# Sums of weight blocks by copies and adding transfers of the DMA, and one pair of modulation vectors summed on VectorE

## The chip, the core and the metric

The kernel runs on one core of a Trainium2 chip. The metric is the device time of one execution in microseconds (us), lower is better. A core has five engines with a queue each, which run in order: TensorE (PE, matrix products into PSUM), VectorE (DVE), ScalarE (ACT), GpSimd (POOL) and SyncE (SP, which here issues transfers). Sixteen DMA engines carry the transfers that SyncE and GpSimd issue.

## What is computed

One inference step of a small two-layer transformer (depth 2, width 1024) over 512 latent tokens and 128 prompt tokens. Each layer has a mixer and a feed-forward part, and both are modulated: six vectors per layer, of which the first two (shift and scale ahead of the mixer) matter here.

```python
def modulation(cond, w_mod, b_mod):
    m = jax.nn.silu(cond) @ w_mod + b_mod              # (1024,) @ (1024, 6 * 1024)
    return m.reshape(cond.shape[:-1] + (N_MOD, D_MODEL))

def trunk_layer(x, mod, p, lam_init, ctx):
    shift1, scale1, gate1, shift2, scale2, gate2 = [mod[:, i][:, None] for i in range(N_MOD)]
    h = rms_norm(x, p["g_pre_mix"]) * (1.0 + scale1) + shift1
    m, own = mixer_block(h, p, lam_init, ctx)
    x = x + gate1 * rms_norm(m, p["g_post_mix"])
    h = rms_norm(x, p["g_pre_ffn"]) * (1.0 + scale2) + shift2
    f = (jax.nn.silu(h @ p["w_gate"]) * (h @ p["w_up"])) @ p["w_down"]   # width 2816
    x = x + gate2 * rms_norm(f, p["g_post_ffn"])
```

All arrays are fp32. There are two conditions, one for the latent tokens and one for the prompt.

## The kernel before

Tokens stand in five tiles of 128 (640 columns, halves of 320). Most products are made of three matmuls on operands split into a high and a low part (`mm3`, `product`): a block of weights is loaded to `raw` (three buffers), ScalarE writes the high half `wh` (L125) and VectorE the low half `wl` (L121), four buffers each (`piece`, L981 to L987). SyncE issues every transfer, in one queue.

The feed-forward part (`ffn`) runs over 22 blocks of the hidden width, taken in pairs, in four groups (`GROUPS`): pairs 0 and 1, then three groups of three. Group 0 is computed plainly. For groups 1 to 3 the gate and up products of a pair use a scheme of seven products instead of eight (`product` with n = 1 to 7, L1046 to L1048), on four weight blocks and on four sums of them; with b11, b12, b21, b22 the blocks of `w_gu`, the sums are b11+b12, b12+b22, b11+b12+b22 and b11+b12+b21+b22, kept in the DRAM tensor `wsum` (quarters 0, 3, 1, 2). Each group ends with its down projection: for two halves of the output and five token tiles, 12 (group 0) or 18 matmuls of 512 columns (L190 to L192) into one of two PSUM banks in turn, evicted by ScalarE in group 0 and added by VectorE (L1200) in the others.

`sums` (L989) is a generator that makes `wsum` for the next group while the current one runs: for each pair and each half of the columns, four loads of 128x512 to `s` buffers (eight of these exist), four adds on VectorE (L1001), four stores (L1002). `step` advances it by one at chosen places: behind three of the plain products, behind a pair, and behind every tile of the down projection. `step(pre, 1, mark)` also says behind which instruction of an engine the new ones are queued: the last one traced so far on the engines named in `mark`, here VectorE.

The modulation vectors are matrix products with two columns (`c2`, the two conditions, padded to 32). Vectors 0 and 1 of layer 1 are made in the feed-forward part of layer 0, in group 1, by `mod_s` (L335): for eight k and four column blocks a load of 128x512 and one plain fp32 matmul (L342) into 32 of the 128 partitions of one bank, 32 in all; `mod_finish` copies the bank out (L258), transposes it in four pieces (L261) and writes the columns `mc` (L268, L270). `middle` advances it at three places within a pair. The order of instructions on each engine is worked out ahead of time by the compiler's scheduler, within the orders that the program asks for.

Of the kernel before, what the change touches and what calls it, by code (L numbers as in the profile page):

```python
# [10 lines left out]
AF = mybir.ActivationFunctionType  # L11
ALU = mybir.AluOpType
# [3 lines left out]
D = 1024  # L16
NT = 5
TOK = NT * 128
KT = D // 128
# [43 lines left out]
class Kernel:  # L63
# [142 lines left out]
    def consts(self):  # L206
        nc, cp, V, G, SY, a = self.nc, self.cp, self.V, self.G, self.SY, self.a
        t = lambda shape, tag, dt=F32: self.tl(cp, shape, tag, 1, dt)

        self.c2 = t([128, 2 * KT + 30], "c2")  # L210
        V.memset(self.c2, 0.0)
        cc = self.c2[:, 0:2 * KT]
        SY.dma_start(cc, a["c2"])
        th = self.tl(self.wp, [128, 2 * KT], "raw", 3)
        self.S.activation(th, cc, AF.Tanh, scale=0.5)
        V.scalar_tensor_tensor(cc, th, 1.0, cc, op0=ALU.add, op1=ALU.mult)
        V.tensor_scalar(cc, cc, 0.5, None, op0=ALU.mult)
# [12 lines left out]
        self.invcnt = t([128, NT, 4], "invcnt")  # L230
        self.gA = t([128, 4, NT, 64], "gA")
        self.mc = t([128, DEPTH, 4, KT, 2], "mc")
        bg = self.tl(self.wp, [128, 1024], "raw", 3)[:, 0:128]
        SY.dma_start(bg, a["mod_bg"])
        p = self.p("pt")[:, 0:128]
        self.T.transpose(p, bg, self.ident)
        self.bgc = t([128, 128], "bgc")
        self.S.activation(self.bgc, p, AF.Copy)

        V.tensor_scalar(self.bgc[:, 96:128], self.bgc[:, 96:128], math.sqrt(D), None, op0=ALU.mult)  # L240
# [91 lines left out]
            return next(raw) if what == "raw" else self.tl(self.pa, [128, 512], "s", NS, dt)  # L332
        return al

    def mod_s(self, l, pair, p, bank):  # L335

        src = self.a["w_mod"][l].rearrange("(k p) (i n) -> p k i n", p=128, n=D)
        for k in range(KT):
            for j in range(4):
                raw = self.s()  # L340
                self.SY.dma_start(raw, src[:, k, pair[j // 2], j % 2 * 512:(j % 2 + 1) * 512])
                self.T.matmul(p[32 * j:32 * j + 32], self.c2[:, 2 * k:2 * k + 32], raw, start=k == 0, stop=k == KT - 1)  # L342
            yield
        self.mod_finish(l, pair, 512, 0, p, lambda what: self.s(), bank)
        yield

    def row(self, l, i, c, tile_):
# [460 lines left out]
    def mixer_e(self, l, first):  # L808
# [7 lines left out]
        pt = lambda dt=F32: self.tl(pa, [128, NT, 256], "PT", 4, dt)  # L816

        def bg():
            if True:
                sets = [self.tl(pa, [128, 3, 1024], tag, n) for tag, n in (("kt", 2), ("kt", 2), ("ka", 1))[:3 - bool(ESTEP[2])]]  # L820
                al = self.mod_alloc(self.ring([x[:, j] for j in range(3) for x in sets]))
                for pair in MODE:
                    p, q = self.pair("s2")
                    yield from self.mod(l, pair, al, p, lambda: q)
        bg = bg()
        step = lambda n: [next(bg, None) for _ in range(n)]
        if not first:
            w = self.win(l, 0, self.es("w0"))
# [4 lines left out]
        for t in range(NT):  # L833
            if first:
                p = first[t]
            else:
                p = self.pg()
# [3 lines left out]
            if t == 4:  # L841
                y = self.tl(pa, [128, 512], "s", NS)
# [3 lines left out]
        w = self.win(l, 1, self.es("w1"))  # L846
# [3 lines left out]
        for t in range(NT):  # L850
            p = self.pg()
# [8 lines left out]
        w = self.win(l, 2, self.es("w2"))  # L860
# [3 lines left out]
        for t in range(NT + 1):  # L864
            if t < NT:
                p = self.pg()
# [8 lines left out]
        w = self.win(l, 3, self.es("w3"))  # L875
# [5 lines left out]
        for t in range(NT + 1):  # L881
            for _ in range(AE[t]):
                self.att(*steps.pop(0))
            if t < NT:
                p = self.p(GX) if GX else self.pg()
# [102 lines left out]

    def sums(self, l, pairs):  # L989

        V, SY = self.V, self.SY
        for pair in pairs:
            for j in range(2):
                c = slice(j * 512, (j + 1) * 512)
                b = [self.s() for _ in range(4)]
                for x, q in zip(b, range(4)):
                    SY.dma_start(x, self.a["w_gu"][l, pair, q][:, c])

                b11, b12, b21, b22 = b
                for q, o, x, y in ((0, b11, b11, b12), (3, b12, b12, b22), (1, b22, b22, b11), (2, b21, b21, b22)):  # L1000
                    V.tensor_tensor(o, x, y, op=ALU.add)  # L1001
                    SY.dma_start(self.a["wsum"][l, pair, q][:, c], o)  # L1002
                yield

    def blocks(self, l, pair):

# [51 lines left out]
    def ffn(self, l, xsrc, xdst, last, m):  # L1058
        a, T, V, S, G, pa = self.a, self.T, self.V, self.S, self.G, self.pa
# [11 lines left out]
        pre = self.sums(l, GROUPS[1])  # L1071
# [21 lines left out]
        for n, (f, h) in enumerate(((0, 0), (1, 0), (0, 1), (1, 1), (2, 0), (2, 1), (3, 0), (3, 1))):  # L1093
            plain(f, h, n)
            if n in (2, 3, 4):
                if n == 2:
                    self.operands()
                with self.behind(self.mark([V, S])):
                    late.append(self.combine(m, *((256, 2, 2), (0, 0, 3), (128, 1, 4))[n - 2]))
            if n > 4:  # L1100
                self.step(pre, 1, self.mark([V]))
        for o, x in late:
            self.split(*o, x, V)
        acc = [x[:, i] for tag, n in (("qa", 2), ("VB", 3))
               for x in [self.tl(pa, [128, n, 1024], tag, 1)] for i in range(n)]

        def mods(gi):
            if l == 0 and gi == 1:
                yield from self.mod_s(1, (1, 0), self.pg(), self.pg)

        def begin(pair):

# [5 lines left out]

        two = lambda x: x.rearrange("p (j n) -> p j n", j=2)

        def middle(st, bg):

            pair, w, aa, x = (st[k] for k in ("pair", "w", "a", "x"))
            b, c = self.p("s2"), self.p("s2")
            wt, yt = self.ptile(), self.ptile()
            t1, t2 = self.ptile(), self.ptile()
            st.update(c=c, t1=t1)
            add = lambda o, p, y: V.tensor_tensor(two(o), p[:, :, n1], two(y), op=ALU.add)  # L1128
            self.product(5, next(w), [b[:, 0], b[:, 1]], last=False)
            add(wt, b, x)  # L1130
            self.product(2, next(w), aa, first=False)
            self.swiglu(t1[:, n1], aa[0][:, n1], aa[1][:, n1], 1, 0)
            next(bg, None)
            self.product(6, next(w), [c[:, 0], c[:, 1]], last=False)
            add(yt, c, x)
            next(bg, None)
            self.product(3, next(w), [b[:, 0], b[:, 1]], first=False)
            add(yt, b, yt)
            self.swiglu(t2[:, n1], yt[:, n1], yt[:, n2], -1, 0)
            next(bg, None)  # L1140
            self.product(7, next(w), [c[:, 0], c[:, 1]], first=False, last=False)
            add(wt, c, wt)
            self.swiglu(t2[:, n2], wt[:, n1], wt[:, n2], -1, 1)
            f = 2 * pair
            ft[f], ft[f + 1] = next(fts), next(fts)
            self.split(ft[f + 1][:, 0], ft[f + 1][:, 1], t2)
            self.split(ft[f][:, 0, n1], ft[f][:, 1, n1], t1[:, n1])
# [8 lines left out]

        for gi, ps in enumerate(GROUPS):
            lastg = gi == len(GROUPS) - 1
            bg = mods(gi)
            st = None  # L1160
            if 0 < gi < len(GROUPS) - 1:
                pre = self.sums(l, GROUPS[gi + 1])
            for pair in ps if gi else ():
                nst = begin(pair)
                if st:
                    end(st)
                st = nst
                middle(st, bg)
                if not lastg and pair != ps[-1]:
                    self.step(pre, 1, self.mark([V]))  # L1170
            for _ in bg:
                pass
            fs = [f for pair in ps for f in (2 * pair, 2 * pair + 1)]
            if lastg:
                rows = [[self.s() for _ in range(2)] for _ in range(2)]
# [5 lines left out]
            for n in range(2):  # L1181
                w = []
                for pair in ps:
                    h, lo = self.piece(a["w_down"][l, n, pair])
                    w += [(h[:, c], lo[:, c]) for c in (slice(0, 512), slice(512, 1024))]
                sl = slice(n * 512, (n + 1) * 512)
                for t in range(NT):
                    c = slice(t * 128, (t + 1) * 128)
                    parts = LC if lastg and last and n == 1 and t == NT - 1 else 1
                    for q in range(parts):  # L1190
                        p = self.pg()[:, 0:512 // parts]
                        b = slice(q * 512 // parts, (q + 1) * 512 // parts)
                        y = acc[t][:, n * 512 + b.start:n * 512 + b.stop]
# [7 lines left out]
                    if st:  # L1201
                        end(st)
                        st = None
                    if not lastg:
                        self.step(pre, 1, self.mark([V]))
                    if lastg:
                        S.activation(self.ptile()[:, 0:512], acc[t][:, sl], AF.Square, accum_out=ss[t][:, n:n + 1])
                        if n == 1:
# [172 lines left out]
```

## Time and profile before

| | |
|---|---|
| median of three runs | 1618.03 us (1617.07 to 1618.66) |
| the profiled execution | 1616.98 us |
| its span, from the first to the last instruction | 1615.2 us |
| mean granted clock of TensorE | 0.985 of full speed |
| bytes moved | 283.89 MB, 176 GB/s over the span |

The profile shows one execution. An engine's busy time is the time in which it executes something; matmuls overlap, so their durations add up to more than their busy time, and the step from one start to the next is what a matmul costs. Layer 0's feed-forward part runs from about 365 to 805 us, layer 1's from about 1172 to 1612 us.

### The profile page before, as it was taken

How to read it: one execution, taken by the hardware profiler on the slowest of the kernel's cores; microseconds unless marked ns; L12 is line 12 of the kernel's file. 1: busy time of each engine (PE TensorE's matmuls, PEld its weight loads, DVE VectorE, ACT ScalarE, POOL GpSimd, SP SyncE). 2: the span in 40 equal slices, each digit the busy share in tenths (PEclk: the TensorE clock that was granted, in tenths of full speed). 3: DMA queues.
4: the chain of work that ended last, by engine and by line, in shares of the span. 5: the costliest groups of instructions: out<-in, count | busy, mean ns of one | idle time of the engine just before them, and what ended most of it. 6: DMA issues, size and time to landing. Idle time of an engine off the chain costs nothing.

```text
span 1615.2 us, 24489 instructions
## 1 busy us (share of the span) xinstructions
PE 1542.9 (96%) x9211; PEld 1296.9 (80%) x9211; DVE 1079.1 (67%) x1891; ACT 716.8 (44%) x1436; POOL 273.2 (17%) x250
## 2 busy tenths in 40 slices
PE   7999989979999999999979999899799999999998
PEld 5676777759877889899867667777598998998996
DVE  4567776786646658757584567766866675775665
ACT  5342676554333224324363426765543441431442
POOL 3124215541000000000140232154510000000002
PEclk9999999989999999999999999999899999999999
DMA  9855020132897687474455541301327877656533
GB/s 328 319 185 165 17 96 22 59 132 92 272 320 249 212 293 257 161 246 158 177 175 179 184 145 50 96 16 51 134 83 253 312 248 251 232 196 235 173 128 130
DMA packets 115030, 283.89 MB, mean 176 GB/s; under 512 B 15312, under 2 KB 26576, under 8 KB 114912
## 3 DMA queue, kind: packets, MB, share of 16 engines
q1 hardware_dynamic: 114912, 282.34, 51.2%
q8 instruction: 72, 1.18, 0.3%
q14 instruction: 46, 0.38, 0.1%
HBM read 233.23 MB, written 49.05 MB: 175 GB/s over the span
## 4 chain that ended last, share of the span: by engine, by line
PE 79%; DVE 6%; POOL 5%; issue 5%; ACT 3%; DMA 2%; SPq 0%; POOLq 0%; DVEq 0%; ACTq 0%
PE s L1048 7%; PE s L1046 7%; PE s L1047 7%; PE g L190 6%; PE g L191 6%; PE g L192 6%; PE o L190 5%; PE o L191 5%; PE o L192 5%; PE s L306 3%; PE pt L1048 3%; PE pt L1046 3%; PE pt L1047 3%; PE s L190 2%; PE s L191 2%
## 5 line engine op out<-in xcount | busy, mean ns | idle before, releaser
L125 ACT ACTIVATE wh<-raw 128x1024 fp32r<-128x1024 f32 (+1 forms) x266 | 243.2, 930 | 342.9 <-PE s L1047 132.3
L121 DVE TENSOR_TENSOR wl<-raw,wh 128x1024 fp32r<-128x1024 f32 (+1 forms) x250 | 281.7, 1135 | 85.1 <-ACT wh L125 82.9
L409 POOL TENSOR_TENSOR qa<-qa,s 128x512 f32<-128x512 f32 x4 | 5.5, 1368 | 807.9 <-DVE wl L121 807.7
L1001 DVE TENSOR_TENSOR s<-s,s 128x512 f32<-128x512 f32 x144 | 98.2, 687 | 48.6 <-DMA s<-in_w_gu 44.1
L190 PE MATMUL g<-wh,hTh 128*128 128x512 f32 x256 | 106.9, 417 | 4.4 <-ACT wh L125 3.8
L191 PE MATMUL g<-wl,hTh 128*128 128x512 f32 x256 | 104.0, 406 | 3.2 <-DVE wl L121 3.2
L576 DVE TENSOR_REDUCE nm<-s 128x1 f32<-128x640 f32 x96 | 77.8, 821 | 40.6 <-PE s L575 21.3
L192 PE MATMUL g<-wh,hTl 128*128 128x512 f32 x256 | 103.4, 404 | 0.0
L1128 DVE TENSOR_TENSOR P<-s,P 128x640 f32<-128x640 f32 x72 | 59.2, 823 | 66.0 <-PE s L1048 66.0
L136 POOL TENSOR_TENSOR rs<-rs,mhalf 128x1 f32<-128x1 f32 (+3 forms) x66 | 59.6, 906 | 195.0 <-DVE rs L133 143.6
L577 ACT ACTIVATE P<-s,nm 128x640 f32<-128x640 f32 x96 | 76.4, 798 | 29.2 <-DVE nm L576 28.0
L1047 PE MATMUL s<-hTl,wh 128*128 128x320 f32 x288 | 89.3, 310 | 0.0
L1046 PE MATMUL s<-kt,wh 128*128 128x320 f32 x288 | 89.2, 310 | 0.0
L1046 PE MATMUL s<-hTh,wh 128*128 128x320 f32 x288 | 89.2, 310 | 0.0
L1048 PE MATMUL s<-hTh,wl 128*128 128x320 f32 x288 | 89.2, 310 | 0.0
L1046 PE MATMUL pt<-hTh,wh 128*128 128x320 f32 x288 | 89.0, 309 | 0.0
L1047 PE MATMUL s<-kt,wh 128*128 128x320 f32 x288 | 89.0, 309 | 0.0
L1048 PE MATMUL s<-kt,wl 128*128 128x320 f32 x288 | 88.9, 309 | 0.0
L1047 PE MATMUL pt<-hTl,wh 128*128 128x320 f32 x288 | 88.8, 309 | 0.0
L1048 PE MATMUL pt<-hTh,wl 128*128 128x320 f32 x288 | 88.0, 309 | 0.0
L190 PEld LDWEIGHTS g<-wh,hTh 128*128 128x128 f32 x256 | 49.5, 193 | 22.3 <-issue 4.6
L190 PE MATMUL o<-wh,hTh 128*128 128x512 f32 x160 | 65.7, 410 | 0.4 <-ACT hTh L125 0.2
(427 smaller groups left out, 4262.8 us busy)
## 6 DMA issues: line engine op xcount, KB each, us to landing
s<-in_w_gu SPq DMA_DIRECT2D x144, 256.0 KB, 4.9
wsum<-s SPq DMA_DIRECT2D x144, 256.0 KB, 4.7
raw<-wsum SPq DMA_DIRECT2D x72, 512.0 KB, 4.7
raw<-in_w_gu SPq DMA_DIRECT2D x70, 512.0 KB, 4.0
kt<-in_w_mod SPq DMA_DIRECT2D x64, 512.0 KB, 6.5
raw<-in_w_down SPq DMA_DIRECT2D x44, 512.0 KB, 3.6
raw<-in_w_in SPq DMA_DIRECT2D x32, 512.0 KB, 6.5
raw<-in_w_out SPq DMA_DIRECT2D x16, 512.0 KB, 4.0
```

Of the source, the lines that this page charges most:

```text
L121: eng.tensor_tensor(lo, src, hi.bitcast(F32), op=ALU.subtract)
L125: self.S.activation(hi, src, AF.Copy)
L136: self.G.tensor_tensor(out, out, self.mhalf[:, :out.shape[-1]], op=ALU.pow)
L190: self.T.matmul(out, ah, bh, start=first, stop=False)
L191: self.T.matmul(out, ah, bl, start=False, stop=False)
L192: self.T.matmul(out, al, bh, start=False, stop=last)
L576: V.tensor_reduce(nm[:, s:s + 1], sc[:, :, :320], axis=AX.XY, op=ALU.max, negate=True)
L577: S.activation(P[s].rearrange("p (a b) -> p a b", a=2), sc[:, :, :320], AF.Exp, bias=nm[:, s:s + 1], accum_out=sm[:, s:s + 1])
L1001: V.tensor_tensor(o, x, y, op=ALU.add)
L1046: self.T.matmul(o, a[0], b[0], start=first and k == 0, stop=False, skip_group_check=True)
L1047: self.T.matmul(o, a[0], b[1], start=False, stop=False, skip_group_check=True)
L1048: self.T.matmul(o, a[1], b[0], start=False, stop=last and k == 3, skip_group_check=True)
```

## The change

Three things change. `sums` no longer uses SBUF and VectorE: per pair it issues four copies of whole blocks (512 KB) from `w_gu` to `wsum` within DRAM on SyncE's queue, and four adding transfers on GpSimd's queue, of which each adds a DRAM block into a block of `wsum`; the four stages of a pair are one step apart, so a group takes n + 3 steps. `mod_s` gives way to `mod_w`: one vector at a time, each load of 128x512 is multiplied by each of the two condition columns on VectorE and added up in four accumulators; at the end four matmuls with `ones` sum them over the partitions, and the result is copied, transposed and written as before. It is advanced behind every second tile of the down projections of groups 0 to 2 in layer 0 (18 steps), queued behind VectorE's and ScalarE's last instruction. And `middle` no longer advances anything. The indexing of `w_mod` and the epilogue of `mod_w` are left out below.

```diff
+        self.ones = t([128, 32], "ones")
+        V.memset(self.ones, 0.0)
+        V.memset(self.ones[:, 0:1], 1.0)
...
-    def mod_s(self, l, pair, p, bank):
-        src = self.a["w_mod"][l].rearrange("(k p) (i n) -> p k i n", p=128, n=D)
+    def mod_w(self, l, i, bank):
...
+        acc = [[self.s() for _ in range(2)] for _ in range(2)]
+        raw = [self.s() for _ in range(4)]
         for k in range(KT):
-            for j in range(4):
-                raw = self.s()
-                self.SY.dma_start(raw, src[:, k, pair[j // 2], j % 2 * 512:(j % 2 + 1) * 512])
-                self.T.matmul(p[32 * j:32 * j + 32], self.c2[:, 2 * k:2 * k + 32], raw, start=k == 0, stop=k == KT - 1)
+            for h in range(2):
+                x = raw[(2 * k + h) % 4]
+                self.SY.dma_start(x, src[:, k, i, h])
+                for c in range(2):
+                    col = self.c2[:, 2 * k + c:2 * k + c + 1]
+                    if k == 0:
+                        V.tensor_scalar(acc[h][c], x, col, None, op0=ALU.mult)
+                    else:
+                        V.scalar_tensor_tensor(acc[h][c], x, col, acc[h][c], op0=ALU.mult, op1=ALU.add)
             yield
-        self.mod_finish(l, pair, 512, 0, p, lambda what: self.s(), bank)
+        p = bank()
+        for h in range(2):
+            for c in range(2):
+                j = 32 * (2 * h + c)
+                T.matmul(p[j:j + 32], self.ones, acc[h][c], start=True, stop=True)
+        b = self.s()
+        self.S.activation(b, p, AF.Copy)
+        q = bank()
+        for k in range(4):
+            T.transpose(q[:, k * 128:(k + 1) * 128], b[:, k * 128:(k + 1) * 128], self.ident)
...
     def sums(self, l, pairs):
-        V, SY = self.V, self.SY
-        for pair in pairs:
-            for j in range(2):
-                c = slice(j * 512, (j + 1) * 512)
-                b = [self.s() for _ in range(4)]
-                for x, q in zip(b, range(4)):
-                    SY.dma_start(x, self.a["w_gu"][l, pair, q][:, c])
-                b11, b12, b21, b22 = b
-                for q, o, x, y in ((0, b11, b11, b12), (3, b12, b12, b22), (1, b22, b22, b11), (2, b21, b21, b22)):
-                    V.tensor_tensor(o, x, y, op=ALU.add)
-                    SY.dma_start(self.a["wsum"][l, pair, q][:, c], o)
-                yield
+        n = len(pairs)
+        for i in range(n + 3):
+            b, w = ([self.a[x][l, pairs[max(0, min(i - d, n - 1))]] for d in range(4)] for x in ("w_gu", "wsum"))
+            add = lambda o, x: self.G.dma_start(o, x, accum_op=ALU.add, max_dma_last_dim=4096)
+            if i < n:
+                for t, q in ((0, 0), (3, 3), (1, 3), (2, 2)):
+                    self.SY.dma_start(w[0][t], b[0][q])
+            if 1 <= i <= n:
+                add(w[1][0], b[1][1])
+                add(w[1][3], b[1][1])
+            if 2 <= i <= n + 1:
+                add(w[2][1], w[2][0])
+            if 3 <= i:
+                add(w[3][2], w[3][1])
+            yield
...
-                self.step(pre, 1, self.mark([V]))
+                self.step(pre, 1, self.mark([self.SY, G]))
...
-        def mods(gi):
-            if l == 0 and gi == 1:
-                yield from self.mod_s(1, (1, 0), self.pg(), self.pg)
+        def mods():
+            for i in ((1, 0) if l == 0 else ()):
+                yield from self.mod_w(1, i, self.pg)
+        bg = mods()
...
-            next(bg, None)                 # three times in middle()
...
-            for _ in bg:
-                pass
...
                     if not lastg:
-                        self.step(pre, 1, self.mark([V]))
+                        self.step(pre, 1, self.mark([self.SY, G]))
+                        if t % 2 == 0:
+                            self.step(bg, 1, self.mark([V, S]))
```

## Rows read from the trace of the kernel before

**Rows 1.** The page's first part: busy us, share of the span, instructions by engine.
```profile
PE 1542.9 (96%) x9211; PEld 1296.9 (80%) x9211; DVE 1079.1 (67%) x1891; ACT 716.8 (44%) x1436; POOL 273.2 (17%) x250
```
**Rows 2.** Busy time by stretch: us, busy us (instructions) of each engine, clock, DMA.
```profile
core 0: us, PE busy (x) PEld busy (x) DVE busy (x) ACT busy (x) POOL busy (x), PEclk, DMA share, GB/s
...
437.00:554.00 117.00, 117.00 (x641) 90.73 (x640) 65.01 (x94) 37.61 (x53) 0.00 (x0) 1.00 0.80 278
554.00:805.00 251.00, 250.89 (x1453) 230.37 (x1452) 171.36 (x239) 87.95 (x123) 5.50 (x5) 1.00 0.62 212
...
1172.00:1612.00 440.00, 435.23 (x2583) 404.44 (x2582) 299.12 (x442) 162.22 (x245) 15.25 (x14) 1.00 0.60 204
```
**Rows 3.** Timeline of PE: start us, us, line, operation, out<-in; one product of L342.
```profile
538.77 0.31 PE L1048 MATMUL s<-hTh,wl 128*128 128x320 f32 x1
539.01 1.05 PE L342 MATMUL g<-s,c 128*32 128x512 f32 x2
539.99 0.41 PE L1046 MATMUL s<-hTh,wh 128*128 128x320 f32 x1
540.24 0.30 PE L1047 MATMUL s<-hTl,wh 128*128 128x320 f32 x1
```
**Rows 4.** Timeline of PE: four products of L342 together.
```profile
458.62 0.31 PE L1048 MATMUL pt<-hTh,wl 128*128 128x320 f32 x1
458.86 1.06 PE L342 MATMUL g<-s,c 128*32 128x512 f32 x8
459.85 0.42 PE L1046 MATMUL s<-kt,wh 128*128 128x320 f32 x1
```
**Rows 5.** Groups by line, 437 to 554 us: busy us, mean ns; idle before, releaser.
```profile
L342 PE MATMUL g<-s,c 128*32 128x512 f32 x64 | 23.1, 605 | 0.0
...
L1001 DVE TENSOR_TENSOR s<-s,s 128x512 f32<-128x512 f32 x19 | 13.0, 687 | 10.2 <-DMA s<-in_w_gu 10.1
```
**Rows 6.** Timeline of PE: before and behind the four transposes of L261.
```profile
543.47 0.31 PE L1048 MATMUL s<-PT,wl 128*128 128x320 f32 x1
...
544.20 0.31 PE L1047 MATMUL s<-PT,wh 128*128 128x320 f32 x1
```
**Rows 7.** Lines L1048, L1200 by layer: ns min/median/max, first and last start us.
```profile
L1048 PE MATMUL pt<-hTh,wl x144: 307/308/414, 440.4 to 766.6; 128*128 128x320 f32 x144
...
L1200 DVE TENSOR_TENSOR qa<-g,qa x6: 683/690/692, 554.1 to 811.2; 128x512 f32<-128x512 f32 x6
...
L1048 PE MATMUL pt<-hTh,wl x144: 307/308/313, 1251.9 to 1551.5; 128*128 128x320 f32 x144
...
L1200 DVE TENSOR_TENSOR qa<-g,qa x6: 683/691/692, 1339.8 to 1595.5; 128x512 f32<-128x512 f32 x6
```
**Rows 8.** Line L1031: the same operation as the new products on VectorE.
```profile
L1031 DVE SCALAR_TENSOR_TENSOR s<-t,s x2: 692/692/692, 403.8 to 1215.4; 128x512 f32<-128x512 f32 x2
```
**Rows 9.** Waits of DVE, 365 to 805 us: us in total, times, longest us.
```profile
DVE s L1001 <- DMA s<-in_w_gu: 23.3, 13, 6.8
```
**Rows 10.** Timeline of POOL, 360 to 830 us: neighbours in the list.
```profile
371.71 1.29 POOL L121 TENSOR_TENSOR hTl<-t,hTh 128x512 fp32r<-128x512 f32 x1 [3.16 <-ACT hTh L125]
790.40 2.81 POOL L409 TENSOR_TENSOR qa<-qa,s 128x512 f32<-128x512 f32 x2 [417.40 <-DVE wl L121]
```
**Rows 11.** Timelines of SP and PE: loads for sums, and a sum's first use.
```profile
389.71 0.33 SPq L997 DMA_DIRECT2D s<-in_w_gu  x1
...
451.72 0.31 PE L1046 MATMUL s<-kt,wh 128*128 128x320 f32 x1
```
**Rows 12.** Transfers, 1260 to 1600 us: packets, MB, share; issues, KB each, us to landing.
```profile
q1 hardware_dynamic: 27381, 70.77, 61.0%
...
wsum<-s SPq DMA_DIRECT2D x52, 256.0 KB, 5.1
s<-in_w_gu SPq DMA_DIRECT2D x48, 256.0 KB, 4.9
```
**Rows 13.** Transfers, 440 to 560 us: GB/s in 40 slices of 3 us.
```profile
GB/s 399 393 391 291 280 315 371 392 320 359 411 378 158 241 220 164 230 286 339 305 392 395 149 157 328 119 161 183 236 287 255 352 249 231 385 283 175 0 0 71
```

More of the change, by code (lines that the diff above doesn't have):

```diff
@@ L333, in mod_alloc @@
         return al
-    def mod_s(self, l, pair, p, bank):
-        src = self.a["w_mod"][l].rearrange("(k p) (i n) -> p k i n", p=128, n=D)
-        for k in range(KT):
-            for j in range(4):
-                raw = self.s()
-                self.SY.dma_start(raw, src[:, k, pair[j // 2], j % 2 * 512:(j % 2 + 1) * 512])
-                self.T.matmul(p[32 * j:32 * j + 32], self.c2[:, 2 * k:2 * k + 32], raw, start=k == 0, stop=k == KT - 1)
-            yield
-        self.mod_finish(l, pair, 512, 0, p, lambda what: self.s(), bank)
+    def mod_w(self, l, i, bank):
+        V, T = self.V, self.T
+        src = self.a["w_mod"][l].rearrange("(k p) (i h n) -> p k i h n", p=128, h=2, n=512)
+        acc = [[self.s() for _ in range(2)] for _ in range(2)]
+        raw = [self.s() for _ in range(4)]
+        for k in range(KT):
+            for h in range(2):
[7 more added lines that the diff above has]
+                        V.scalar_tensor_tensor(acc[h][c], x, col, acc[h][c], op0=ALU.mult, op1=ALU.add)
+            yield
+        p = bank()
[8 more added lines that the diff above has]
+            T.transpose(q[:, k * 128:(k + 1) * 128], b[:, k * 128:(k + 1) * 128], self.ident)
+        q = q.rearrange("p (k h c r) -> p h k c r", h=2, c=2, r=32)
+        m = self.mc[:, l, self.COLS[i]].rearrange("p (h k) c -> p h k c", h=2)
+        col = lambda j: self.bgc[:, j:j + KT].rearrange("p (h k) -> p h k", h=2).unsqueeze(3) \
+            .to_broadcast([128, 2, 4, 2])
+        V.tensor_tensor(m, q[:, :, :, :, 0], col(48 * l + 8 * i), op=ALU.add)
+        if i % 3 == 1:
+            V.scalar_tensor_tensor(m, m, 1.0, col(96 + 16 * (i // 3) + 8 * l), op0=ALU.add, op1=ALU.mult)
         yield
@@ L818, in bg @@
         def bg():
-            if True:
                 sets = [self.tl(pa, [128, 3, 1024], tag, n) for tag, n in (("kt", 2), ("kt", 2), ("ka", 1))[:3 - bool(ESTEP[2])]]
@@ L1119, in ffn, with middle @@
         two = lambda x: x.rearrange("p (j n) -> p j n", j=2)
-        def middle(st, bg):
+        def middle(st):
             pair, w, aa, x = (st[k] for k in ("pair", "w", "a", "x"))
@@ L1132, in middle @@
             self.swiglu(t1[:, n1], aa[0][:, n1], aa[1][:, n1], 1, 0)
-            next(bg, None)
             self.product(6, next(w), [c[:, 0], c[:, 1]], last=False)
             add(yt, c, x)
-            next(bg, None)
             self.product(3, next(w), [b[:, 0], b[:, 1]], first=False)
@@ L1139, in middle @@
             self.swiglu(t2[:, n1], yt[:, n1], yt[:, n2], -1, 0)
-            next(bg, None)
             self.product(7, next(w), [c[:, 0], c[:, 1]], first=False, last=False)
@@ L1158, in ffn @@
             lastg = gi == len(GROUPS) - 1
-            bg = mods(gi)
             st = None
@@ L1167, in ffn @@
                 st = nst
-                middle(st, bg)
+                middle(st)
                 if not lastg and pair != ps[-1]:
-                    self.step(pre, 1, self.mark([V]))
-            for _ in bg:
-                pass
+                    self.step(pre, 1, self.mark([self.SY, G]))
             fs = [f for pair in ps for f in (2 * pair, 2 * pair + 1)]
@@ L1204, in ffn @@
                     if not lastg:
-                        self.step(pre, 1, self.mark([V]))
+                        self.step(pre, 1, self.mark([self.SY, G]))
+                        if t % 2 == 0:
+                            self.step(bg, 1, self.mark([V, S]))
                     if lastg:
```

## Prediction

> **What bounds the kernel now.** I began with the busy times [rows 1]: TensorE 96%, VectorE 67%, ScalarE 44%, GpSimd 17%. An average hides stages, so the second view was busy time by stretch [rows 2]. In the two feed-forward stages TensorE is busy for 117.00 of 117 us, 250.89 of 251 us and 435.23 of 440 us, all at the full granted clock (1.00, 2.4 GHz). So there no wait of VectorE, of SyncE or of a transfer reaches the end of the program: whatever TensorE doesn't have to execute is saved in full, and whatever another engine stops doing is worth nothing until TensorE waits for it. The third view was the order of TensorE's instructions. In the pair stages its matmuls of 320 columns start every 0.147 us; the only breaks are the plain fp32 matmuls of `mod_s` (L342) [rows 3, 4].
>
> **What comes off TensorE.** In [rows 3] one product of L342 (two records) stands between two ordinary ones: from the start at 538.77 to the second ordinary start behind it at 540.24 are 1.47 us, where two steps of 0.147 us would be 0.29. The break costs 1.18 us. In [rows 4] four products (eight records) stand together, in the four 32-column groups: 1.06 us against 1.05 us, so four cost what one costs. L342 was busy 23.1 us [rows 5]; at 1.05 us each those are 22 breaks for 32 products, so most stood alone. 22 times 1.18 is 26.0 us. The four transposes of `mod_finish` [rows 6] take from 543.47 to 544.20, 0.73 us for two steps of 0.147: 0.44 us more. Together 26.4 us. A second way to the same term: the two layers run the same program in this stage but for `mod_s`. From the first L1048 to the first eviction of the group (L1200) layer 0 takes 554.1 - 440.4 = 113.7 us, layer 1 1339.8 - 1251.9 = 87.9 us [rows 7]. The difference is 25.8 us. I take 26.0.
>
> **What comes onto TensorE.** Each of the two vectors now has four products with `ones` and four transposes. The products cost one break if they stand together (1.18 us) and four if they stand alone (4.72). Their four operands get ready one VectorE instruction apart, 0.69 us [rows 8], which is less than a product's 1.05 us, so I expect them in two breaks: 2.36 us. With 0.44 for the transposes that is 2.8 us a vector, 5.6 for both; bounds 3.2 and 10.3. These products add a wait, too: TensorE for the last VectorE product. Behind it stand the matmuls of the next tile. The trace has no such wait; the nearest thing, TensorE waiting on VectorE or ScalarE in these stages, hardly exists (0.11 us idle in 251 [rows 2]), so between 0 and 3 us a vector; I take 0.5 each, near the row. Net: 26.0 - 5.6 - 1.0 = 19.4 us saved.
>
> **What moves to VectorE.** 8 k times 2 halves times 2 columns times 2 vectors are 64 products of 128x512, at 0.69 us [rows 8] 44 us, in 18 steps of four (2.8 us) placed behind the eviction of every second tile of the down projection. Removed are 144 adds at 0.687 us [rows 5], 99 us. So VectorE's load falls even in layer 0 (72 adds, 49 us, against 44), and it was not the bound: I cost both at nothing, hidden by TensorE's matmuls. The cover: a tile of a later group is 18 matmuls of 0.234 us, 4.2 us, and two PSUM banks alternate, so VectorE may come one tile late without stopping TensorE. A step of 2.8 us and an eviction of 0.69 leave some 5 us of the 8.4 us of two tiles for a late `w_mod` load. The adds of before waited for their loads 13 times, 23.3 us in all, at most 6.8 us [rows 9], without a mark on TensorE. Behind a waiting product on VectorE stand the evictions (L1200) and the low halves of weights (L121).
>
> **What moves to the DMA.** Per pair eight loads and eight stores of 256 KB become four copies and four adding transfers of 512 KB: the bytes moved are the same. The copies go out from SyncE, where nothing waits for VectorE any more; the adds from GpSimd, idle from 371.71 to 790.40 us in layer 0 [rows 10], so its issue time and its waits for copies cost nothing; behind them only further adds are queued. The new wait is SyncE's: a load `raw<-wsum` waits for an adding transfer, and every other weight load is queued behind it. How early is the sum needed? The first loads of sums go out at 389.71 and TensorE first uses a summed block (the keys `s<-kt`, product 5) at 451.72 [rows 11]: 62 us for one copy (about 5 us) and one add. For a later group there are 116 us for twelve adds, 9.7 us each even if they ran one after the other.
>
> How long an adding transfer takes, this trace can't say. Take its time per byte as f times that of a copy. From 1260 to 1600 us q1 was busy 61.0% of 340 us, 207 us, for 70.77 MB; the sums were 52 + 48 transfers of 0.262 MB, 26.2 MB, so 77 us, and the rest 130 us [rows 12]. Half of the 77 become copies (38), half adds: 130 + 38 + 38 f. At f = 1 nothing changes; at f = 2, an add reading two streams where a copy reads one, it is 244 of 340 us; it fills the stretch at f = 4.5. I take f = 2: no cost. A gain from fewer, larger packets has no path to TensorE either.
>
> A row and a rule differ here on the ceiling. In slices of 3 us the queue moved up to 411 GB/s [rows 13]. The Trainium skill (DMA: Bandwidth & Descriptors, Bandwidth) puts the memory's share of one core at about 358 GB/s. Counting each added byte as two reads and a write, and each copied one as a read and a write, the stretch would move 110 MB, 308 of 340 us at that rate: no cost, but so near the limit that my chance for the second rival below would be 0.20. The trace's own slice is above that limit, so I don't use it.
>
> Edits with one answer: `ones` and its two memsets (VectorE is idle at the start), the dropped `for _ in bg` loop: nothing.
>
> **The sum.** The profiled execution took 1616.98 us (span 1615.2, 1.8 around it). 1616.98 - 19.4 = 1597.6. The median of the three runs is 1618.03, 1.05 above the profiled one: 1598.6, which I round to 1598.5. If everything goes at the good ends (3.2 us added, no wait) it is 1618.03 - 22.8 = 1595.2.
>
> **The rivals.**
> 1. *VectorE falls behind the w_mod loads*: 18 steps, each with four loads of x through SyncE's one queue, behind weight loads that wait for buffers. Where a load is over 5 us late the eviction is late and TensorE stops. For it: waits up to 6.8 us [rows 9], and in the first group's down projection, tiles of 2.8 us. Against it: the adds stood in the same places with the same waits. Six such steps at 2 us are 12 us: 1610.5; with the bad end of the products (10.3) up to 1615.
> 2. *The adding transfers become the bound*, and the kernel gets slower: it decides at f = 4.5, place: the pair stages of groups 1 to 3 in both layers, where SyncE stands at `raw<-wsum`. At f = 5 the stretch needs 358 us, 18 more than it has; at 5.5, 37 more; two layers at 5.5: 1598.5 + 74 = 1672. For it: q1 is already at 0.80 in layer 0 [rows 2]. Against it: a factor over 4 would be needed.
> 3. *The freed VectorE and SyncE time also counts*: only if TensorE had waited for them; its idle time in these stages is under 1 us outside the first microseconds [rows 2]. 1592 to 1595 at best.
> 4. *The change doesn't take off what it says* (the new products scattered and waited for, ordinary matmuls delayed as long): 1618.
>
> **How the numbers follow.** Forecast (1594.5 to 1602.5) 0.65; rival 1 (1602.5 to 1615) 0.18; rival 2 (above 1622) 0.10; rival 3 0.04; rival 4 0.03. The range leaves out the slow case, rival 4 and the tail of rival 1: 1592 to 1612. About 0.2% (3.2 us) is what a measurement here can tell from no change. Faster by more: 0.65 + 0.18 + 0.04 = 0.87; within: 0.03; slower: 0.10.
>
> **What would show it.** Right: the stage from the first L1048 to the first L1200 of the group lasts about 88 us in both layers; TensorE has 16 records of the new products instead of 64; its busy share in the feed-forward stages stays at 100%; layer 1's stage keeps its 440 us. Wrong: idle time of TensorE in front of L190 behind VectorE's eviction (rival 1), or in front of the pair products with ScalarE's splits waiting for `raw<-wsum` and SyncE at that load (rival 2); the latter would show in both layers alike.

## The result and the profile after

The changed kernel is slower: 1628.75 us (median of four, 1627.04 to 1631.1) against 1617.74 us of the kernel before on the same chip, a ratio of 1.0068 with a 95% interval of 1.0055 to 1.008. The profiled execution took 1627.1 us, its span 1625.3 us. The forecast was 1598.5 us.

In the new file the matmuls of `product` stand on L1077 to L1079 (before: L1046 to L1048), the weight load `raw` on L1013, the copies of `sums` on L1026 and its adds on L1023, the down projection's evictions on L1224 (ScalarE, group 0) and L1226 (VectorE), and the products with `ones` on L362.

The page's first part and its queues, after (queue: packets, MB, share of 16 engines' time); the first row answers to [rows 1]:

```profile
PE 1534.0 (94%) x9167; PEld 1299.9 (80%) x9167; DVE 1029.4 (63%) x1813; ACT 713.3 (44%) x1437; POOL 334.5 (21%) x322
...
q1 hardware_dynamic: 75744, 244.57, 42.9%
q0 software_dynamic: 10368, 37.75, 12.7%
```

TensorE is busy 8.9 us less than before and the span is 10.1 us longer: it lost work and gained idle time. q0 is GpSimd's queue, the adding transfers alone. The stretches of [rows 2], after:

```profile
core 0: us, PE busy (x) PEld busy (x) DVE busy (x) ACT busy (x) POOL busy (x), PEclk, DMA share, GB/s
...
437.00:554.00 117.00, 114.44 (x669) 105.22 (x668) 77.59 (x111) 42.41 (x60) 9.84 (x12) 0.99 0.84 246
554.00:805.00 251.00, 247.71 (x1436) 225.94 (x1435) 163.23 (x230) 87.01 (x125) 17.35 (x18) 0.99 0.65 203
...
1172.00:1612.00 440.00, 428.80 (x2512) 395.04 (x2511) 241.79 (x346) 154.35 (x230) 39.91 (x45) 0.99 0.66 194
```

Before, TensorE filled all three, but for 5 us of the third. Layer 1 has no modulation work in either kernel; what it loses is lost to the sums alone.

To measure layers apart I take one landmark stretch in each: from the last start of group 0's plain products (L190 `s<-hTh,wh`) to the last start of the down projection's adds into `VB`. In layer 1 these are the rows below, first before, then after (ns min/median/max, first and last start).

```profile
L190 PE MATMUL s<-hTh,wh x80: 309/309/634, 1171.9 to 1230.6; 128*128 128x320 f32 x80
L1200 DVE TENSOR_TENSOR VB<-g,VB x10: 424/691/692, 1349.7 to 1608.1; 128x512 f32<-128x512 f32 x9, 128x256 f32<-128x256 f32 x1
```

```profile
L190 PE MATMUL s<-hTh,wh x80: 309/309/632, 1165.2 to 1224.4; 128*128 128x320 f32 x80
L1226 DVE TENSOR_TENSOR VB<-g,VB x10: 425/692/692, 1355.8 to 1617.9; 128x512 f32<-128x512 f32 x9, 128x256 f32<-128x256 f32 x1
```

1608.1 - 1230.6 = 377.5 us became 1617.9 - 1224.4 = 393.5 us. In layer 0 the same stretch went from 406.8 to 399.8 us. That is -7.0 and +16.0; the rest of the program adds 1.1, which makes the span's 10.1. (In layer 0 the last add into `VB` is one from bank `o`, not `g`.)

**Where in layer 1.** Slices of 20 us, after (columns as above):

```profile
1224.00:1244.00 20.00, 14.41 (x54) 10.97 (x53) 8.45 (x14) 7.05 (x14) 1.64 (x2) 0.83 0.85 238
...
1284.00:1304.00 20.00, 19.03 (x128) 18.51 (x128) 13.43 (x22) 8.72 (x14) 2.47 (x3) 1.00 0.99 291
1304.00:1324.00 20.00, 17.57 (x116) 16.78 (x115) 12.30 (x17) 8.76 (x13) 1.63 (x2) 1.00 0.93 232
...
1364.00:1384.00 20.00, 20.00 (x93) 16.48 (x92) 4.37 (x6) 2.19 (x3) 0.00 (x0) 1.00 0.14 49
```

With 1404 to 1444 (18.66 and 19.12 busy at DMA shares of 0.96 and 0.94) these are all the slices from 1224 to 1604 us in which TensorE stands still; their idle time adds up to 11.2 us. None has a DMA share under 0.85, while the stretch as a whole has 0.64 and slices of 0.14 lie between. The engines of the DMA are full in bursts. Not every full slice loses time: 1264 to 1284 us has 0.93 and 1384 to 1404 has 0.98, and TensorE fills both.

The largest stop, read backwards through four engines (timelines of SyncE, ScalarE and TensorE after; in brackets the idle time before the instruction, and what ended it):

```profile
1217.98 0.33 SPq L1013 DMA_DIRECT2D raw<-in_w_down  x1
...
1234.55 1.06 ACT L125 ACTIVATE wh<-raw 128x1024 fp32r<-128x1024 f32 x1 [5.00 <-DMA raw<-in_w_down]
1235.51 0.42 ACT L1084 ACTIVATE P<-s 128x320 f32<-128x320 f32 x1
1235.83 0.59 ACT L1224 ACTIVATE qa<-g 128x512 f32<-128x512 f32 x1
...
1236.47 0.79 PE L190 MATMUL g<-wh,t 128*128 128x512 f32 x1 [5.34 <-ACT qa L1224]
1237.06 0.63 PE L191 MATMUL g<-wl,t 128*128 128x512 f32 x1
```

A block of `w_down` is asked for at 1217.98 and can be split at 1234.55: 16.6 us. Before, the load at the same place was split after 14.0 us, and ScalarE didn't wait for it:

```profile
1217.66 0.33 SPq L984 DMA_DIRECT2D raw<-in_w_down  x1
...
1231.70 1.05 ACT L125 ACTIVATE wh<-raw 128x1024 fp32r<-128x1024 f32 x1
```

So the load had a cover of some 14 us there, where the median of such loads landed in 3.6. After, ScalarE stands at that split; the eviction that would free a PSUM bank is queued behind it; TensorE stands 5.34 us at the bank. When it goes on, its matmuls start 0.43 us apart up to 1241.26 instead of 0.234: in that stretch the granted clock is 0.51, the lower of the two levels (1.2 GHz), and from 1241.49 it is 1.00 again. Eleven steps at 0.43 instead of 0.234 are 2.2 us more for this one stop.

The second largest stop, in a pair stage, has no eviction in it: a load of `w_gu` keeps ScalarE waiting, and TensorE stands at the split itself.

```profile
1305.63 1.06 ACT L125 ACTIVATE wh<-raw 128x1024 fp32r<-128x1024 f32 x1 [5.58 <-DMA raw<-in_w_gu]
...
1306.74 0.42 PE L1077 MATMUL pt<-hTh,wh 128*128 128x320 f32 x1 [1.75 <-ACT wh L125]
```

The sum for layer 1: TensorE's idle time in the landmark stretch is 393.5 - 382.28 = 11.2 us (before 377.5 - 376.98 = 0.5), and the same matmuls take 5.3 us more busy time. 10.7 + 5.3 = 16.0. Of the 5.3 the stop at the PSUM bank has 2.2; the rest isn't the granted clock, which is 1.00 in every other slice up to 1604 us, and isn't traced to single stops.

What waits for what, after: ScalarE's splits (us in total, times, longest), and the issues of the page's last part (KB each, median us to landing).

```profile
ACT wh L125 <- DMA raw<-in_w_gu: 57.9, 22, 9.1
...
ACT wh L125 <- DMA raw<-wsum: 57.4, 27, 4.7
...
ACT wh L125 <- DMA raw<-in_w_down: 29.6, 8, 8.4
```

```profile
wsum<-in_w_gu SPq DMA_DIRECT2D x72, 512.0 KB, 7.4
raw<-wsum SPq DMA_DIRECT2D x72, 512.0 KB, 4.8
raw<-in_w_gu SPq DMA_DIRECT2D x70, 512.0 KB, 5.0
...
raw<-in_w_down SPq DMA_DIRECT2D x44, 512.0 KB, 8.1
wsum<-in_w_gu POOLq DMA_DIRECT2D x36, 512.0 KB, 10.9
wsum<-wsum POOLq DMA_DIRECT2D x36, 512.0 KB, 7.6
```

Before, ScalarE waited 7.7 us for `in_w_gu`, 5.0 for `wsum` and had no wait for `in_w_down` in its list; the loads landed in 4.0, 4.7 and 3.6 us. These landings are medians of the few loads for which the trace gives one: after, 8 of the 70 of `in_w_gu`, 7 of the 72 of `wsum` and 6 of the 44 of `in_w_down`, the last all in layer 0. The waits count every split.

**What came out as foreseen.** In the timeline of TensorE the four products with `ones` stand together (the count is of records, two to a product):

```profile
555.13 0.40 PE L192 MATMUL g<-wh,ka 128*128 128x512 f32 x1
555.46 1.06 PE L362 MATMUL o<-s,ones 128*32 128x512 f32 x8
556.67 0.41 PE L1077 MATMUL pt<-hTh,wh 128*128 128x320 f32 x1 [0.15 <-ACT wh L125]
```

And the stage of [rows 7], first layer 0, then layer 1, after:

```profile
L1079 PE MATMUL pt<-hTh,wl x144: 307/308/392, 451.6 to 761.1; 128*128 128x320 f32 x144
L1226 DVE TENSOR_TENSOR qa<-g,qa x6: 687/692/692, 540.4 to 805.7; 128x512 f32<-128x512 f32 x6
...
L1079 PE MATMUL pt<-hTh,wl x144: 305/309/416, 1253.3 to 1561.4; 128*128 128x320 f32 x144
L1226 DVE TENSOR_TENSOR qa<-g,qa x6: 691/692/692, 1345.9 to 1605.3; 128x512 f32<-128x512 f32 x6
```

Layer 0: 540.4 - 451.6 = 88.8 us, where it was 113.7 and 88 were forecast. Layer 1: 92.6 us, where 87.9 were to stay.

### The profile page after: what moved, and what is told of

It is laid out like the page before. It is cut to its first block, busy times and chain, and to the rows that moved or that the text cites. A ratio compares the mean times of both kernels' runs of the same rounds, so it can differ in the third digit from the quotient of the medians.

```text
span 1625.3 us, 24058 instructions
## 1 busy us (share of the span) xinstructions
PE 1534.0 (94%) x9167; PEld 1299.9 (80%) x9167; DVE 1029.4 (63%) x1813; ACT 713.3 (44%) x1437; POOL 334.5 (21%) x322
## 3 DMA queue, kind: packets, MB, share of 16 engines
q0 software_dynamic: 10368, 37.75, 12.7%
## 4 chain that ended last, share of the span: by engine, by line
PE 61%; DMA 14%; DVE 9%; issue 6%; ACT 5%; POOL 4%; SPq 0%; POOLq 0%; DVEq 0%; ACTq 0%
DMA raw<-wsum 7%; PE g L190 6%; PE g L191 6%; PE g L192 6%; PE o L190 5%; PE o L191 5%; PE o L192 5%; PE s L1079 4%; PE s L1077 4%; PE s L1078 4%; DMA raw<-in_w_down 3%; PE s L310 3%; DVE wl L121 3%; ACT wh L125 2%; POOL wh L127 2%
## 5 line engine op out<-in xcount | busy, mean ns | idle before, releaser
L190 PE MATMUL g<-wh,hTh 128*128 128x512 f32 x256 | 106.6, 416 | 3.2 <-ACT wh L125 2.7
L1023 POOL DMA_DIRECT2D wsum<-in_w_gu x36 | 29.9, 847 | 312.4 <-DMA wsum<-in_w_gu 299.2
L1077 PE MATMUL s<-hTh,wh 128*128 128x320 f32 x288 | 90.2, 313 | 3.4 <-ACT wh L125 1.8
L1079 PE MATMUL s<-kt,wl 128*128 128x320 f32 x288 | 89.6, 311 | 2.7 <-DVE wl L121 2.7
L1077 PE MATMUL pt<-hTh,wh 128*128 128x320 f32 x288 | 89.3, 311 | 2.4 <-ACT wh L125 2.3
L1077 PE MATMUL s<-kt,wh 128*128 128x320 f32 x288 | 89.2, 310 | 1.4 <-DVE P L1160 1.1
L1079 PE MATMUL s<-hTh,wl 128*128 128x320 f32 x288 | 89.7, 311 | 0.7 <-DVE wl L121 0.7
L1079 PE MATMUL pt<-hTh,wl 128*128 128x320 f32 x288 | 87.7, 310 | 0.8 <-DVE wl L121 0.8
L1023 POOL DMA_DIRECT2D wsum<-wsum x36 | 29.6, 822 | 222.5 <-DMA wsum<-wsum 112.7
L190 PEld LDWEIGHTS g<-wh,hTh 128*128 128x128 f32 x256 | 49.4, 193 | 21.2 <-ACT wh L125 3.7
L190 PE MATMUL o<-wh,hTh 128*128 128x512 f32 x160 | 65.6, 410 | 0.5 <-ACT hTh L125 0.2
## 6 DMA issues: line engine op xcount, KB each, us to landing
wsum<-in_w_gu POOLq DMA_DIRECT2D x36, 512.0 KB, 10.9
```

What stands on the lines that cost most here:

```text
L190: self.T.matmul(out, ah, bh, start=first, stop=False)
L1023: add = lambda o, x: self.G.dma_start(o, x, accum_op=ALU.add, max_dma_last_dim=4096)
L1077: self.T.matmul(o, a[0], b[0], start=first and k == 0, stop=False, skip_group_check=True)
L1079: self.T.matmul(o, a[1], b[0], start=False, stop=last and k == 3, skip_group_check=True)
```

## The experiments

The theory (T): the modulation part saves some 23 us in layer 0, and the sums by DMA cost some 16 us in each layer, because the adding transfers make other weight loads late. Rivals: the modulation part doesn't save what it should, VectorE being the limit (M); SyncE's queue is held up by the copies (Q); the loads of sums wait for the chain of copy, add and add (D). The table has the medians, the ratio to the kernel before as timed beside each run (medians from 1617.74 to 1618.47 us), and from each profiled execution the median landing of a `w_down` load, ScalarE's waits for `w_down` loads in layer 1 (us in total, 1172 to 1640 us) and the two landmark stretches. The landings rest on 17 to 20 loads in before, e1, e3 and e8 and on 3 to 6 in the others, where, but for two in e7, all are in layer 0; so they say little of layer 1, and the waits say more.

| kernel | us | ratio to before, 95% | `in_w_down` lands, us | waits for `in_w_down`, layer 1 | layer 0 | layer 1 |
|---|---|---|---|---|---|---|
| before | 1617.74 | | 3.6 | none | 406.8 | 377.5 |
| after | 1628.75 | 1.0055 to 1.008 | 8.1 | 18.3 | 399.8 | 393.5 |
| e1, modulation alone | 1639.05 | 1.0111 to 1.0154 | 3.5 | none | 427.7 | 378.3 |
| e8, the same, products later | 1620.19 | 0.9999 to 1.0033 | 3.6 | none | 406.7 | 377.5 |
| e2, sums alone | 1641.23 | 1.0134 to 1.0165 | 12.6 | 21.6 | 414.3 | 395.0 |
| e3, no sums made | 1593.71 | 0.9836 to 0.9869 | 3.5 | none | 383.7 | 376.7 |
| e4, copies, no adds | 1592.48 | 0.9831 to 0.986 | 4.2 | none | 383.9 | 376.8 |
| e5, adds made plain copies | 1593.21 | 0.983 to 0.9879 | 5.2 | 4.9 | 383.2 | 376.9 |
| e9, no load waits for a sum | 1628.49 | 1.005 to 1.0104 | 7.0 | 20.9 | 402.9 | 398.6 |
| e7, sums spread out | 1601.44 | 0.9877 to 0.992 | 3.6 | 5.1 | 387.5 | 376.8 |

(The profiled execution of e9 took 1639.7 us, above its median; so its stretches are longer than those of a median run.)

### One part of the change at a time

e2 is the changed kernel with `mod_s` put back as it was. e1 is the kernel before with `mod_w` in place of `mod_s`; as `sums` still uses the `s` buffers there, the accumulators lie in another tile (`gA`) and a vector is made in two halves, two products with `ones` each:

```diff
+        g = self.gA.rearrange("p a t e -> p (a t e)")
+        for h in range(2):
+            acc = [g[:, c * 512:(c + 1) * 512] for c in range(2)]
...
+                if k % 2 and k < KT - 1:
+                    yield
+            p = bank()
+            for c in range(2):
+                T.matmul(p[32 * c:32 * c + 32], self.ones, acc[c], start=True, stop=True)
```

> The kernel before, with only the modulation part of the change; its accumulators lie in the mixer's unused table gA (two of them, so a vector is made in two halves), because the eight s buffers belong to the sums, which stay on VectorE. Theory T (the transfers of the sums come in bursts that fill the DMA engines, and weights land late): without them the forecast's first term holds. TensorE loses 26.0 us and gets four times (two products in one or two breaks of 1.18 us, 0.44 us of transposes), 6.5 to 11.2 us: 15 to 19.5 us faster than before, about 1600. Rival M (VectorE's products and their loads hold up evictions): 1610 or more, with TensorE idle behind VectorE's evictions in layer 0's down projections.

> The changed kernel with the old mod_s in place of mod_w: only the sums are made by copies and adding transfers. T: the loss is all theirs, and mod_s costs what the new form saved, about 20 us: 1645 to 1652; both layers' feed-forward stages are longer than before, layer 1's by about 16 us as in the changed kernel. M: the loss comes with the new products; 1617 to 1630 then.

The sums alone cost 23 us, 17.5 in layer 1 and 7.5 in layer 0; T expected 1645 to 1652. The two parts don't simply add up in layer 0: with the old `mod_s` the sums cost 7.5 us there, in the changed kernel 16.1 (399.8 against e3's 383.7). The modulation part alone didn't save anything: 1639.05. The trace of e1 says where (waits of TensorE from 365 to 840 us, and the stretch 437 to 554):

```profile
PE o L358 <- DVE gA L353: 16.4, 1, 16.4
```

```profile
437.00:554.00 117.00, 101.64 (x614) 93.12 (x612) 93.57 (x141) 39.33 (x56) 0.00 (x0) 0.96 0.77 271
```

TensorE stands 16.4 us once, at the products with `ones`, for VectorE's last product (the granted clock is 0.50 from 543.8 to 567.7, around this stop): in e1 the products follow in the same step as the last VectorE work, while VectorE has the adds of the old `sums` to do as well, 93.57 us of 117. e8 puts the products one step later and is the same otherwise.

```diff
-                if k % 2 and k < KT - 1:
+                if k % 2:
                     yield
...
+        if not i:
             yield
```

> The kernel with the modulation part alone again (sums on VectorE as before), but the products with ones come one step (two token tiles) later. In the first such kernel TensorE stood for 16 us in front of the first of them, waiting for VectorE's last product, and its clock fell. If that wait was its loss (1639), it is gone: 1598 to 1608. If VectorE simply has too much to do with the adds and the products (M), 1620 or more, with TensorE idle elsewhere behind VectorE.

The stall is gone, and the gain is still missing: 1620.19, layer 0 at 406.7 as before. Its waits in layer 0, and the same stretch:

```profile
PE g L363 <- ACT s L360: 4.9, 2, 3.5
PE pt L1074 <- DVE wl L121: 4.6, 2, 3.7
```

```profile
437.00:554.00 117.00, 111.31 (x661) 101.72 (x659) 95.57 (x144) 42.84 (x60) 0.00 (x0) 1.00 0.80 277
```

TensorE now waits for the low halves of weights (`wl`) on VectorE, busy 95.57 of 117 us (before 65.01 [rows 2], after 77.59). In layer 0's stretch it stands idle for 13.1 us, against 1.2 in e3; that is half of the 23.0 us by which e8's stretch is longer. The other half is busy time: for 10.2 us of the stretch the granted clock was 0.50 (555.0 to 558.4 and 664.3 to 671.1), and vectors made in halves have two more breaks, some 3 us by [rows 3] and [rows 6] (an estimate); the rest isn't traced. So M is right for this part by itself, as far as the idle time goes: VectorE has room for `mod_w` only because the sums left it. In the changed kernel, where both parts stand, TensorE doesn't wait for VectorE's products: in front of L362 it stands 0.4 us for a `wl` and 0.2 us for nothing that the profile shows.

### Which part of the sums

e3 issues neither copies nor adds, and its loads of sums read blocks of `w_gu`; e4 keeps the copies and leaves out the adds; e5 turns the adds into plain copies on the same queue, with the same waits:

```diff
-            add = lambda o, x: self.G.dma_start(o, x, accum_op=ALU.add, max_dma_last_dim=4096)
+            add = lambda o, x: self.G.dma_start(o, x, max_dma_last_dim=4096)
```

> The changed kernel with no sums made at all; the loads of sums read the raw blocks of w_gu instead (as many loads of the same size), so the pair products are computed on other weights. T, and Q (the copies stand in SyncE's queue ahead of weight loads): everything lost comes back, TensorE waits for nothing, 1595 to 1600. Rival O (the compiler's order of the instructions has become worse, or M): 1610 or more, TensorE idle at the same places.

> The changed kernel with the copies on SyncE but no adding transfers (the sums stay incomplete). In the changed kernel q0 took 5.5 us per MB and q1 2.9, so the adds are two thirds of the sums' time on the DMA engines. T: most of the loss goes: 1600 to 1608. Q (the copies in SyncE's queue are the cause): hardly better than the changed kernel, 1620 to 1628.

> The changed kernel with the adding transfers turned into plain copies of the same blocks on GpSimd's queue, with all their waits (so no sums are made). Theory T (an adding transfer holds the DMA engines 2.2 times as long as a copy, 5.5 us per MB against 2.5, and in bursts this makes weight loads late): q0's time per MB falls to 2.5 to 3, and most of the loss of the adds (1628.75 against 1592.5 with the copies alone, 36 us) goes: 1594 to 1606. Rival D (what hurts is not the engines' time but the chain copy, add, add, load, through GpSimd's queue and its waits): hardly changed, 1618 to 1628.

1593 us each time, and 377 us in layer 1. So the modulation part saves 406.8 - 383.7 = 23.1 us in layer 0, the copies cost nothing (Q falls), and as many bytes in as many transfers on GpSimd's queue, issued by the same waits, cost nothing either: the loss belongs to adding. All three came out 1 to 8 us below the range that T gave them, e4 by most: T had put a part of the loss on the copies, and they have none. The share of that queue in e5:

```profile
q0 software_dynamic: 10368, 37.75, 6.7%
```

6.7% of e5's span of 1591.2 us are 107 us for 37.75 MB, 2.8 us per MB; the adds take 12.7% of 1625.3, 206 us, 5.5 us per MB. With e4's and e3's q1 (44.7% of 1593.1 us less 38.8% of 1591.4, for 37.75 MB more) a copy costs 2.5 us per MB. An add takes 1.9 to 2.2 times what a copy takes. No run gives plain copies that much engine time (twice as many of them, say), so e5 by itself doesn't tell the time on the engines from the adding.

e5 also shows that one late load isn't enough. The first `w_down` load of layer 1 there is asked for at 1178.50 and split 16.8 us later, and yet TensorE has no wait from 1160 us to the end of the stretch:

```profile
1178.50 0.47 SPq L1013 DMA_DIRECT2D raw<-in_w_down  x1
...
1195.29 1.06 ACT L125 ACTIVATE wh<-raw 128x1024 fp32r<-128x1024 f32 x1 [4.92 <-DMA raw<-in_w_down]
```

The fourth, the one that stopped the changed kernel, is split 10.3 us after its issue there (1197.64 to 1207.93), without a wait.

### The chain of sums, or the engines

e9 keeps every copy and add, but no load waits for a sum: all loads read `w_gu`.

```diff
-        for x in (b[0], w[0], b[2], w[1], b[3], w[3], w[2]):
+        for x in (b[0], b[0], b[2], b[1], b[3], b[3], b[2]):
```

> The changed kernel with all its copies and adds, but the loads of sums read blocks of w_gu (other weights), so that no load waits for a copy or an add. T: the engines are as full, hence nothing gained: 1620 to 1630. D: the loss goes with the wait: 1593 to 1603.

1628.49 us, what the changed kernel takes. D falls: the loss doesn't need a load that waits for a sum. What is left is that the adds run in the engines while other loads do.

### The same transfers, spread out

e7 makes the same sums in the same tensor, one copy and its add per step: four steps within each pair of groups 1 and 2, and none in the down projections of these groups. In group 0 the twelve steps begin behind the second plain product, and the last five fall in its down projection.

```diff
+        for pair in pairs:
+            b, w = self.a["w_gu"][l, pair], self.a["wsum"][l, pair]
+            for t, q, x in ((0, 0, b[1]), (3, 3, b[1]), (1, 3, w[0]), (2, 2, w[1])):
+                self.SY.dma_start(w[t], b[q])
+                self.G.dma_start(w[t], x, accum_op=ALU.add, max_dma_last_dim=4096)
+                yield
...
+            self.step(pre, 1, self.mark([self.SY, G]))
             self.product(2, next(w), aa, first=False)
```

> The changed kernel with the same copies and adds, but spread: one copy and the add that goes with it in a step, four steps in each pair of groups 1 and 2 (between its products), and from the second plain product on in group 0. T: the same time on the DMA engines without bursts; weight loads land in 4 to 6 us instead of 8, and 15 to 30 us of the loss go: 1598 to 1613. D: the chain is as long and now ends later; 1625 or more.

1601.44 us: 1.0% faster than the kernel before, 1.7% faster than the changed one. Its queue, its loads of `w_down`, and three slices of layer 1:

```profile
q0 software_dynamic: 10368, 37.75, 12.6%
...
raw<-in_w_down SPq DMA_DIRECT2D x44, 512.0 KB, 3.6
```

```profile
1216.00:1236.00 20.00, 20.00 (x92) 16.48 (x91) 7.80 (x11) 9.37 (x15) 3.16 (x4) 1.00 0.91 257
1236.00:1256.00 20.00, 20.00 (x113) 18.05 (x112) 5.48 (x5) 7.65 (x12) 1.80 (x3) 1.00 0.95 240
...
1276.00:1296.00 20.00, 20.00 (x138) 20.00 (x137) 14.06 (x22) 8.54 (x13) 2.48 (x3) 1.00 0.99 307
```

The adds take the engine time that they took (12.6%), the engines are as full in these slices as in the bad ones of the changed kernel, and TensorE fills every one; layer 1 is back at 376.8 us. So neither a full DMA nor the time of the adds is by itself the loss; how they are arranged is. The waits in the table part the kernels: where ScalarE waits for `w_down` loads of layer 1 for 5.1 us or less, the layer loses nothing; where it waits for 18.3 us or more, the layer loses 16 us and up. The landings don't part them as well: e7's `in_w_gu` loads took 6.9 us (ten of 70), the changed kernel's 5.0.

What the arrangement has to be isn't settled. The down projection as a place isn't it, for group 0 at least: the first two slices above lie mostly in e7's (1217 to 1249 us), and four copies and five adds are issued in it without a stop; in the changed kernel's (1225 to 1265 us) only two adds are, and there TensorE stopped for 5.34 us. From the issue of the first to the split of the last of group 0's four `w_down` loads the changed kernel issues eight adds in 37.0 us and e7 five in 33.5. In the pair stages the changed kernel lets four copies go at once (L1026, 3.12 us from 1289.57), ahead of the stop at 1306.74, where e7 sends them one at a time between the loads. That fewer transfers at once make the difference is argued from these rows: e7 also changes the places, and no run parts the two. Some 8 us up to e3's 1593.7 are left in e7; its layer 0 is 4 us longer than e3's, and the rest isn't placed.

## Why the prediction was wrong

**What bounds the kernel: right.** TensorE filled the feed-forward stages, and what was taken off it was saved in full wherever nothing else was added (e3 to e5).

**Off and onto TensorE: right in kind, a little small.** 26.0 off fits what the runs show; onto it came one break a vector, not two, and waits of 0.6 us. The forecast netted 19.4, its good end 22.8, the runs show 23.1. I had taken the time at which each operand gets ready for the time at which its product is executed, so two breaks; all four stand together, as those of [rows 4] did.

**VectorE at nothing: right for the sum of the parts, wrong as a statement on this part.** The forecast costed the 64 products and the 144 removed adds together. e1 and e8 show that without the removal VectorE takes the gain back. Rival 1 didn't occur.

**What moves to the DMA: this is the step that failed.** "I take f = 2: no cost." The factor was right: 1.9 to 2.2. So was the load on the stretch: 244 of 340 us were forecast, and the transfers of 1260 to 1600 us, after, say

```profile
q1 hardware_dynamic: 12031, 53.61, 44.5%
q0 software_dynamic: 3456, 12.58, 20.7%
```

65.2%, 222 us. What failed is the conclusion from it: the adds cost 16.0 us in layer 1 and 16.1 in layer 0, not nothing. I asked whether the stretch has room for the transfers, and whether a sum is ready when needed; the answer to both was yes, and e9 shows that the second doesn't matter. I didn't ask how late the *other* loads get while adds are in the engines. Their cover is three `raw` buffers and ScalarE's lead, some 14 us for the load above, and in the changed kernel the first of group 0's four loads in layer 1 was split 18.1 us after its issue (1197.58 to 1215.64) and the fourth 16.6 us. The unit to judge by was the loads in a burst, not the mean of 340 us. The row that could have warned me is [rows 13], where slices of 3 us vary from 0 to 411 GB/s: the queue was bursty already.

**"Behind them only further adds are queued" was true of GpSimd's queue and beside the point.** The Trainium skill (DMA: Bandwidth & Descriptors, Issuing engines are not separate DMA queues) states that transfers of all issuing engines run on the same 16 DMA engines and interleave there. The traces agree: adds issued by GpSimd moved the landing of SyncE's `w_down` loads from 4.2 us (e4) to 8.1 us (medians of six loads each, in layer 0).

The ceiling that I set aside I had read without its condition. The Trainium skill (DMA: Bandwidth & Descriptors, Bandwidth) gives about 358 GB/s as a core's share when both cores of a memory are streaming, and has 425 GB/s measured with one of them idle; the 411 GB/s of [rows 13] lie under that, so row and rule don't differ. No run here shows either figure to bind: e7's slice at 307 GB/s and a DMA share of 0.99 costs nothing, and the changed kernel's slices lose time at 232 to 303 GB/s.

**Rival 2 named the right transfers and the wrong mechanism.** It wanted f above 4.5, SyncE at `raw<-wsum`, and a loss of 18 us and more a layer. In the changed kernel the loss came alike in both layers, as it said, but at f of about 2, and in e9 just as well, where no load waits for a sum; SyncE's waits for transfers into `wsum` are some 10 us in all of layer 1. Its chance of 0.10 was low because its price rested on the mean as well.

**The sum as measured.** 1617.7 - 23.1 + 16.1 (layer 0: 399.8 - 383.7) + 16.0 + 1.1 = 1627.8, against 1628.75. The 23.1 and the 16.1 both hang on e3's layer 0; measured in the changed kernel itself is only their difference, the 7.0 us by which layer 0 became shorter.

## To carry to other kernels

Before work is moved to the DMA, ask not only whether the stage's mean leaves room but how late the loads get that are issued in the middle of the new transfers, and compare that with the lead of their consumers (buffers ahead, and what is queued in order behind the consumer). Spread such transfers one at a time over the stretch: here the same transfers went from a loss of 0.7% to a gain of 1.0%. And an engine's room is to be judged for each part of a change by itself, if the parts may be taken apart.

## What the hardware showed that I had not expected

An adding transfer from DRAM into DRAM took 5.5 us of all 16 engines per MB, a plain one 2.5 to 2.8; a block of 512 KB landed 7.6 to 10.9 us after its issue (medians; as plain copies in e5: 5.0 to 8.2). Full DMA engines didn't stop TensorE by themselves: at shares of 0.91 to 0.99 over 20 us e7's TensorE didn't wait at all. And one stop of 5.34 us of TensorE was followed by 4.79 us at a granted clock of 0.51, the lower level, so it cost 2.2 us beyond itself.
